# A preparation's inputs in another place, a new order of its TensorE work, and a gate bias loaded as rows

## The chip, the cores and the metric

The kernel runs on one core of one Trainium2 chip. The metric is the device time of one execution in microseconds; the time before is 2539.73 us, the median of three runs (2536.66 to 2539.75).

## The reference, cut to what matters

One layer works on x of 1024 tokens by 1024 channels, all in float32:

```
x = x + 0.5 * swiglu(rmsnorm(x, ff1_norm), ff1_w_gate, ff1_w_up, ff1_w_down)   # d_ff = 2816
h = rmsnorm(x, mix_norm)
a_in, q, k, v, g_logits = split(h @ w_in)
y_a = gmlp_spatial_gating(gelu(a_in), ...)
y_b = stick_breaking_attention(q, k, v)          # 16 heads of 64, strictly causal
g_a, g_b = split(sigmoid(g_logits + b_gate))     # b_gate: 2 * 1024
x = x + (g_a * (y_a @ w_branch_a) + g_b * (y_b @ w_branch_b)) @ w_out
x = x + 0.5 * swiglu(rmsnorm(x, ff2_norm), ff2_w_gate, ff2_w_up, ff2_w_down)
y = rmsnorm(x, final_norm)
```

## The kernel before, in words

Each float32 operand is split into a high and a low part (ScalarE casts the high part, VectorE or GpSimd subtracts it to get the low one), and each product is three matmuls: high times high, high times low, low times high (lines 67 to 69 for the mixer, 166 to 168 for the layer halves).

The program has three stages. `ffn` runs twice, as the first layer half (f1) and as the second (f2); `mixer` stands between them.

`ffn` multiplies by a Strassen-Winograd scheme with seven products instead of eight. It begins with a **preparation**. The eight row blocks t of x (128 tokens each) are normalized (`normed`, line 111: sum of squares on ScalarE, a power on GpSimd, one half of the row scaled on VectorE at line 116, the other multiplied by the weights on GpSimd at line 114 and scaled on ScalarE at line 117) and transposed on TensorE (line 177) into right operands: B11 and B21 from blocks 0 to 3 (`lo_forms`), and B22, T3, T1, T2, T4 from blocks 4 to 7 (`hi_forms`). For each of the blocks 4 to 7, `hi_forms` transposes first, and leaves two later steps, `second` and `third`. These add or subtract B11 or B21 with matmuls by a plus or minus unit matrix (line 199), each followed by a split into a T (lines 185 and 186); each step on the same bank can begin only when the split before it has read the bank.

Between these pieces TensorE works on **heads**: head f is the product of 128 columns of the gate weights with B11 (`pb`) and with B21 (`ba`), which `head_part` issues as parts of 12 matmuls of 512 columns (or two half parts of 256). The heads 0 to 3 are made in the preparation. After that `tail(f)` does the other products with T1 to T4 and B22 for each f, 22 in all, and stores sums for the second phase, the products with `wd` (tiles pf, wf, pd). In f1 all eight blocks are prepared; in f2 (`ready`) B11 and B21 come from the mixer, and only blocks 4 to 7 are left. The x of f2 is xres, which the mixer stores at its end (line 828).

In the preparation the order of TensorE and of SyncE, which issues all DMAs, is the written one; instructions written outside may still be placed between them. ScalarE, VectorE and GpSimd follow an order that a planner chooses at build time, each engine then in that order; outside such blocks it orders TensorE and SyncE as well, and may take an instruction ahead of earlier ones when its operands and buffers are free. An operand's buffer can be taken over tile by tile from a pool that has ended (`reuse_waits="tile"`).

The space of SBUF is a stack. Below lie `hp` (four operands of 16 KB per partition) and `wp` (two raw weight tiles, six forms wf). On these stands, in the layer halves, `bp` (two more raw tiles and two more forms, 16 KB), then `tp` (T3, T4 and B22, 48 KB), `pg` (8 KB) and on top `pre` (gain, three x tiles, xn, diff) and after it `pa` (the tails' tiles, 38 KB). For the second phase `pb` stands where tp, pg and pa stood. In the mixer `gp` (eight tiles of 2 KB for the v of attention, gates and parts of m) stands where bp stands, and on it attention's pool `ap` (90 KB) and, after attention, `u2` (42 tiles of 2 KB) and `np2` (10 KB and little tiles) in the same place.

In the mixer, banks of PSUM have tags: z and later projections use p0 (three banks), projections of q, k, v and the gates A use p1 (two), transposes p2 (two). The gates of the first four d are called before gMLP and write into gp, so they can run while attention does; their sigmoid (line 776) adds `bgate`, a tile that line 765 loads with 128 partitions of 16 single elements each.

Of the kernel before, what the change touches and what calls it, by code (L numbers as in the profile page):

```python
# [19 lines left out]
HALF = 512  # L20
# [3 lines left out]
XNF, XNB = 7, 5  # L24
# [8 lines left out]
class Kernel:  # L33
# [74 lines left out]
        nc.gpsimd.tensor_tensor(r[:, 1:2], r[:, 0:1], self.neghalf, op=ALU.pow)  # L108
        return r[:, 1:2]

    def normed(self, x, gain, tiles):

        nc = self.nc
        nc.gpsimd.tensor_tensor(tiles[1], x[1], gain[1], op=ALU.mult)  # L114
        r = self.rstd(x, tiles[0])
        nc.vector.scalar_tensor_tensor(tiles[0], x[0], r, gain[0], op0=ALU.mult, op1=ALU.mult)
        nc.scalar.activation(tiles[1], tiles[1], AF.Copy, scale=r)

    def gain(self, g):
        t = [self.utile("gain") for _ in range(2)]  # L120
# [102 lines left out]
    def ffn(self, xsrc, gain_src, wg, wu, wd, before, after, T=None):  # L223
# [13 lines left out]
        with ExitStack() as outer:  # L237
            fps = outer.enter_context(tc.tile_pool(name="fps", bufs=8, space=PSUM, reuse_waits="tile"))
            self.psum = lambda tag, name: fps.tile([P, HALF], F32, tag="ps", name=name)
            bp = outer.enter_context(tc.tile_pool(name="bp", bufs=1, reuse_waits="tile"))  # L240
            count = {"raw": 0, "wf": 0}

            def rawt():
                count["raw"] += 1
                own = count["raw"] % 2 == 0
                return (bp if own else self.wp).tile([P, D], F32, tag="raw", bufs=2, name="raw")

            def wform(src, sub=None):
                count["wf"] += 1
                own = count["wf"] % 4 == 0  # L250
                return self.form(bp if own else self.wp, "wf", 2 if own else 6, src, sub)


            with tc.tile_pool(name="tp", bufs=3, reuse_waits="tile") as tp, tc.tile_pool(name="pg", bufs=1, reuse_waits="tile") as pg:
                T = T or self.first_forms()
                for i, n in enumerate(("T2", "T1", "T3", "T4", "B22")):
                    T[n] = (self.hp if i < 2 else tp).tile([P, 4, 2, HALF], F32R, tag="h", name=n)
# [30 lines left out]
                    tt(glo, a, glo, op=ALU.add)  # L288
                    return gate, b, glo

                with tc.tile_pool(name="pre", bufs=1, reuse_waits="tile") as pre, tc.manual_schedule(engines={mybir.EngineType.PE, mybir.EngineType.SP}):
# [3 lines left out]
                    x, heads = {}, {}  # L295

                    def load(t):
                        x[t] = pre.tile([P, D], F32, tag="xr", bufs=3, name="xr")
                        nc.sync.dma_start(out=x[t], in_=xsrc[t * P:(t + 1) * P, :])

                    def norm(t):
                        xn = [tmp("xn", 4) for _ in range(2)]
                        self.normed(cut(x[t]), cut(gain), xn)
                        return xn

                    pool = nc.gpsimd.tensor_tensor
                    q = [slice(i * 256, (i + 1) * 256) for i in range(2)]
                    full = lambda f: heads.update({f: head_end(heads[f])})
                    if ready:
                        heads[0], heads[1] = head(0, pool), head(1, pool)  # L310
                        nc.sync.dma_start(out=gain, in_=gain_src.partition_broadcast(P))
                        for t in (4, 5, 6):
                            load(t)
                        work = {4: 0, 5: 1, 6: 2, 7: 3}
                    else:
                        load(0)
                        nc.sync.dma_start(out=gain, in_=gain_src.partition_broadcast(P))
                        load(1), load(2)
                        heads[0] = head(0, pool)
                        load(3)  # L320
                        heads[1] = head(1, pool)
                        self.lo_forms(0, norm(0), T)
                        self.lo_forms(1, norm(1), T)
                        head_part(heads[0], q[0])
                        load(4)
                        self.lo_forms(2, norm(2), T)
                        head_part(heads[1], q[0])
                        load(5)
                        self.lo_forms(3, norm(3), T)
                        load(6)  # L330
                        for f in range(2):
                            head_part(heads[f], q[1])
                            full(f)
                        work = {4: 2, 5: 3}
                    for t in range(4, NT):
                        f = work.get(t)
                        if f is not None and f not in heads:
                            heads[f] = head(f, pool)
                        xn = norm(t)
                        if ready:  # L340
                            head_part(heads[f], which=(2,))
                        second, third = self.hi_forms(t, xn, T, tmp)
                        if t == 4:
                            load(7)
                        if f is not None:
                            head_part(heads[f], which=(3,) if ready else (2,))
                            if ready:
                                full(f)
                        second()
                        if f is not None and not ready:  # L350
                            head_part(heads[f], which=(3,))
                            full(f)
                        third()

                with tc.tile_pool(name="pa", bufs=1, reuse_waits="tile") as pa:
                    tile = lambda tag, bufs: pa.tile([P, HALF], F32, tag=tag, bufs=bufs, name=tag)

# [55 lines left out]
                    for f in range(nff):  # L413
                        if f not in heads:
                            heads[f] = head(f)
                            head_part(heads[f])
                            full(f)
# [460 lines left out]
```

## Time and profile before

| | |
|---|---|
| median of three runs | 2539.73 us |
| the profiled execution | 2541.97 us |
| its span, from the first to the last instruction | 2540.2 us |
| TensorE matmul busy | 2451.0 us |
| VectorE, ScalarE, GpSimd busy | 1685.2, 1050.4, 350.0 us |
| mean granted clock of TensorE | 0.986 of full speed |
| preparation of f1, attention, preparation of f2 | from 0, to 1268.5, from 1851.5 us |

Busy time counts an instruction from its start to its modelled end; matmuls overlap, so a stretch in which TensorE is busy throughout can hold more or less work. In a timeline, a row gives start, length, engine, line and operation, and in brackets the idle time before it and what ended that.

### The profile page before, as it was taken

What the parts mean: (1) busy time and instruction counts of PE and PEld (TensorE: products, weight loads), DVE (VectorE), ACT (ScalarE), POOL (GpSimd) and SP (SyncE); (2) the same over time, 40 slices, a digit from 0 to 9 for tenths busy, and PEclk for the clock granted to TensorE, in tenths of its full rate; (3) what the DMA queues carried; (4) which work ended last, traced back from release to release, by engine and by line L of the source; (5) the groups of instructions that cost most, each with busy time, mean ns of one, the idle gap of its engine ahead of it and who ended that gap; (6) DMA issues with size and microseconds to landing.
All of it is one profiled execution on the core that took longest, in us unless ns stands there. A gap on an engine that the chain in (4) does not pass through costs nothing.

```text
span 2540.2 us, 33329 instructions
## 1 busy us (share of the span) xinstructions
PE 2451.0 (96%) x12268; PEld 2074.1 (82%) x12268; DVE 1685.2 (66%) x2595; ACT 1050.4 (41%) x1996; POOL 350.0 (14%) x510
## 2 busy tenths in 40 slices
PE   6999999999999999999999999999979999999998
PEld 5788888788889897988888888888857888887886
DVE  5877787565757888787675555145848777874655
ACT  6333333344646666665522222222334333333444
POOL 4000000000324445443200000000130000000002
PEclk9999999999999999999999999999989999999999
DMA  4553553775421212121111121123445535547653
GB/s 145 181 171 124 177 176 128 292 253 173 157 58 34 67 34 67 34 67 51 34 51 53 47 71 58 54 75 125 133 129 178 175 126 178 173 138 285 229 178 133
DMA packets 252771, 318.33 MB, mean 125 GB/s; under 512 B 14912, under 2 KB 172096, under 8 KB 252608
## 3 DMA queue, kind: packets, MB, share of 16 engines
q1 hardware_dynamic: 252608, 316.21, 38.4%
q8 instruction: 96, 1.57, 0.3%
q14 instruction: 67, 0.55, 0.1%
HBM read 227.55 MB, written 80.22 MB: 121 GB/s over the span
## 4 chain that ended last, share of the span: by engine, by line
PE 83%; DVE 7%; DMA 4%; issue 2%; ACT 1%; POOL 1%; SPq 0%; POOLq 0%; DVEq 0%; ACTq 0%
PE pj L67 7%; PE pj L68 7%; PE pj L69 7%; PE pd L168 7%; PE pd L167 7%; PE pd L166 7%; PE pb L167 4%; PE pb L166 4%; PE pb L168 4%; PE av L609 3%; PE pv L68 2%; PE pv L69 2%; PE pv L67 2%; PE tr L602 2%; PE pe L167 1%
## 5 line engine op out<-in xcount | busy, mean ns | idle before, releaser
L150 ACT CAST wf<-raw 128x512 fp32r<-128x512 f32 x280 | 166.7, 620 | 237.2 <-PE pd L168 99.1
L67 PE MATMUL pj<-h,wf 128*128 128x512 f32 x640 | 254.6, 398 | 5.7 <-DVE q L74 5.7
L151 DVE TENSOR_TENSOR wf<-raw,wf 128x512 fp32r<-128x512 f32 x264 | 178.0, 696 | 118.0 <-ACT wf L150 115.7
L68 PE MATMUL pj<-h,wf 128*128 128x512 f32 x640 | 253.3, 396 | 0.0
L69 PE MATMUL pj<-h,wf 128*128 128x512 f32 x640 | 252.8, 396 | 0.0
L57 DVE TENSOR_TENSOR wf<-raw,wf 128x1024 fp32r<-128x1024 f32 x88 | 108.3, 1231 | 143.3 <-ACT wf L56 142.8
L585 DVE TENSOR_TENSOR_SCAN kp<-kp 128x128 f32<-128x128 f32 (+7 forms) x128 | 179.9, 1413 | 33.5 <-POOL kp L583 32.0
L150 ACT CAST wf<-ws 128x512 fp32r<-128x512 f32 x176 | 107.9, 622 | 207.8 <-DVE ws L159 106.5
L56 ACT CAST wf<-raw 128x1024 fp32r<-128x1024 f32 x88 | 92.8, 1054 | 222.0 <-PE pj L68 121.1
L589 POOL TENSOR_TENSOR bt<-bt,kp 128x512 f32<-128x512 f32 (+4 forms) x128 | 129.8, 1015 | 139.9 <-DVE kp L585 119.4
L67 PEld LDWEIGHTS pj<-h,wf 128*128 128x128 f32 x640 | 122.1, 191 | 31.2 <-DVE q L74 7.0
L67 PE MATMUL pv<-wf,h 128*128 128x256 f32 x512 | 145.1, 285 | 2.1 <-ACT vg L652 2.1
L68 PE MATMUL pv<-wf,h 128*128 128x256 f32 x512 | 145.3, 284 | 0.6 <-DVE wf L57 0.6
L69 PE MATMUL pv<-wf,h 128*128 128x256 f32 x512 | 145.3, 284 | 0.0
L69 PEld LDWEIGHTS pj<-h,wf 128*128 128x128 f32 x640 | 121.9, 190 | 25.0 <-DVE wf L57 0.2
L68 PEld LDWEIGHTS pj<-h,wf 128*128 128x128 f32 x640 | 122.2, 191 | 24.2
L114 POOL TENSOR_TENSOR xn<-x,gain 128x512 f32<-128x512 f32 x12 | 16.8, 1406 | 893.9 <-DVE x L474 601.6
L166 PE MATMUL pb<-T,wf 128*128 128x512 f32 x352 | 137.5, 391 | 0.8 <-ACT pe L372 0.8
L167 PE MATMUL pb<-T,wf 128*128 128x512 f32 x352 | 137.0, 389 | 0.0
L168 PE MATMUL pb<-T,wf 128*128 128x512 f32 x352 | 136.9, 389 | 0.0
L166 PE MATMUL pd<-wf 128*128 128x512 f32 x344 | 133.1, 394 | 1.8 <-DVE x L463 1.6
L167 PE MATMUL pd<-wf 128*128 128x512 f32 x344 | 134.6, 391 | 0.0
(216 smaller groups left out, 6585.1 us busy)
## 6 DMA issues: line engine op xcount, KB each, us to landing
raw<-in_ff_w_down_dram SPq DMA_DIRECT2D x66, 512.0 KB, 6.3
raw<-in_w_in_dram SPq DMA_DIRECT2D x56, 512.0 KB, 3.9
raw<-in_ff_w_gate_dram SPq DMA_DIRECT2D x52, 512.0 KB, 4.4
raw<-in_ff_w_up_dram SPq DMA_DIRECT2D x44, 512.0 KB, 6.0
f_t2t<-as SPq DMA_DIRECT2D x22, 512.0 KB, 4.9
f_a11a<-act SPq DMA_DIRECT2D x44, 256.0 KB, 4.2
f_s2s<-as SPq DMA_DIRECT2D x22, 512.0 KB, 2.7
f_s3s<-as SPq DMA_DIRECT2D x22, 512.0 KB, 5.6
```

What stands on the lines that cost most here:

```text
L56: nc.scalar.copy(hi, raw)
L57: (nc.gpsimd if early else nc.vector).tensor_tensor(lo, raw, hi.bitcast(F32), op=ALU.subtract)
L67: mm(ps, lhsT=lh, rhs=rh, start=first, stop=False)
L68: mm(ps, lhsT=lh, rhs=rl, start=False, stop=False)
L69: mm(ps, lhsT=ll, rhs=rh, start=False, stop=last)
L150: self.nc.scalar.copy(f[:, 0, :], src)
L151: (sub or self.nc.vector.tensor_tensor)(f[:, 1, :], src, f[:, 0, :].bitcast(F32), op=ALU.subtract)
L166: mm(ps, lhsT=lh, rhs=rh, start=first, stop=False, skip_group_check=True)
L167: mm(ps, lhsT=lh, rhs=rl, start=False, stop=False, skip_group_check=True)
L168: mm(ps, lhsT=ll, rhs=rh, start=False, stop=last, skip_group_check=True)
L585: nc.vector.tensor_tensor_scan(rev, rev, rev, 1.0, op0=ALU.mult, op1=ALU.bypass)
L589: eng.tensor_tensor(bt[:, :n], bt[:, :n], kp[:, i * HALF + 1:i * HALF + 1 + n], op=ALU.mult)
```

## The change

Five edits. (1) Gain and the x tiles of a preparation get a pool `xp` of their own, which opens first, where gp stands in the mixer; `pre` keeps xn and diff, and `bp` opens only when both have closed, so that the preparation has two raw tiles and six forms instead of four and eight. (2) `tp` and `pg` stand at the other end of SBUF (`side="right"`). (3) For blocks 0 and 1 the second half of the row is normalized by one VectorE instruction. (4) TensorE and SyncE get a new order in the preparation: in f2 both parts of head 0 come before the first transposes, the third step of a block comes after the first of the next block, heads 2 and 3 lie one block later than in f1 before; in f1 the first two x tiles are loaded before gain. (5) `b_gate` is no longer loaded at the beginning of the mixer but behind attention, into a tile of np2 as 16 rows of 128, which TensorE transposes and VectorE copies to `bgate`.

```diff
-    def normed(self, x, gain, tiles):
+    def normed(self, x, gain, tiles, shared=True):
-        nc.gpsimd.tensor_tensor(tiles[1], x[1], gain[1], op=ALU.mult)
+        if shared:
+            nc.gpsimd.tensor_tensor(tiles[1], x[1], gain[1], op=ALU.mult)
         r = self.rstd(x, tiles[0])
         nc.vector.scalar_tensor_tensor(tiles[0], x[0], r, gain[0], op0=ALU.mult, op1=ALU.mult)
-        nc.scalar.activation(tiles[1], tiles[1], AF.Copy, scale=r)
+        if shared:
+            nc.scalar.activation(tiles[1], tiles[1], AF.Copy, scale=r)
+        else:
+            nc.vector.scalar_tensor_tensor(tiles[1], x[1], r, gain[1], op0=ALU.mult, op1=ALU.mult)
...
-            bp = outer.enter_context(tc.tile_pool(name="bp", bufs=1, reuse_waits="tile"))
-            count = {"raw": 0, "wf": 0}
+            bp, count = None, {"raw": 0, "wf": 0}
...
-                own = count["wf"] % 4 == 0
+                own = bp and count["wf"] % 4 == 0
...
-            with tc.tile_pool(name="tp", bufs=3, reuse_waits="tile") as tp, tc.tile_pool(name="pg", bufs=1, reuse_waits="tile") as pg:
+            right = lambda name, bufs: tc.tile_pool(name=name, bufs=bufs, side="right", reuse_waits="tile")
+            with right("tp", 3) as tp, right("pg", 1) as pg:
...
+                left = lambda name: tc.tile_pool(name=name, bufs=1, reuse_waits="tile")
+                with left("xp") as xp, left("pre") as pre, tc.manual_schedule(engines={mybir.EngineType.PE, mybir.EngineType.SP}):
-                    gain = pre.tile([P, D], F32, tag="gain", name="gain")
+                    gain = xp.tile([P, D], F32, tag="gain", name="gain")
...
                     if ready:
-                        heads[0], heads[1] = head(0, pool), head(1, pool)
-                        nc.sync.dma_start(out=gain, in_=gain_src.partition_broadcast(P))
-                        for t in (4, 5, 6):
-                            load(t)
+                        new_head(0)
+                        load_gain()
+                        load(4), load(5)
+                        new_head(1)
+                        load(6)
+                        norm(4)
+                        part(0, 2), part(0, 3)
                     else:
-                        load(0)
-                        nc.sync.dma_start(out=gain, in_=gain_src.partition_broadcast(P))
-                        load(1), load(2)
+                        load(0), load(1)
+                        load_gain()
+                        load(2)
...
+                    first(4)
+                    load(7)
+                    norm(5)
+                    if ready:
+                        part(1, 2)
+                        second(4)
+                        new_head(2)
+                        part(1, 3)
+                    else:
+                        part(1, 2, q[1])
+                        second(4)
+                        new_head(2)
+                        part(1, 3, q[1])
+                    first(5)
+                    norm(6)
+                    third(4)
+                    new_head(3)
+                    part(2, 2)
+                    second(5)
+                    part(2, 3)
+                    first(6)
+                    norm(7)
+                    third(5)
+                    part(3, 2)
+                    second(6)
+                    part(3, 3)
+                    first(7)
+                    third(6)
+                    second(7)
+                    third(7)
+
+                bp = outer.enter_context(left("bp"))
...
-        nc.sync.dma_start(out=bgate, in_=a["b_gate"][0].rearrange("(c p) -> p c", p=P))
         with tc.tile_pool(name="attn", bufs=2, reuse_waits="tile") as ap:
             self.attention(ap, ydram)
         with tc.tile_pool(name="u2", ...) as self.up, tc.tile_pool(name="np2", ...) as self.np_:
+            rows = self.np_.tile([16, P], F32, tag="xn", bufs=XNB, name="rows")
+            nc.sync.dma_start(out=rows, in_=a["b_gate"][0].rearrange("(c p) -> c p", p=P))
+            ps = self.psum("p2", "bg")
+            nc.tensor.transpose(ps[:, :16], rows, self.ident[:16, :16])
+            nc.vector.tensor_copy(bgate, ps[:, :16])
```

`first(t)` calls `hi_forms`, `second(t)` and `third(t)` its two later steps, and `part(f, n, cs)` is `head_part` for pb (n = 2) or ba (n = 3), over all 512 columns or over the half q[0] or q[1]. In f1, ahead of `first(4)`, the blocks 0 to 3 alternate with half parts of the heads 0 and 1.

## Rows read from the trace of the kernel before

**Rows 1.** The page, part 1: busy us, share of the span, instructions.
```profile
PE 2451.0 (96%) x12268; PEld 2074.1 (82%) x12268; DVE 1685.2 (66%) x2595; ACT 1050.4 (41%) x1996; POOL 350.0 (14%) x510
```

**Rows 2.** TensorE's waits, whole span: for whom, us in total, times, longest.
```profile
PE nt L177 <- DVE xn L116: 19.9, 3, 10.6
PE nt L199 <- DVE T L186: 14.5, 7, 4.7
PE pd L167 <- DVE pf L151: 8.1, 3, 3.1
...
PE pv L67 <- ACT vg L652: 2.1, 1, 2.1
```

**Rows 3.** Stretches: length, busy us of PE, PEld, DVE, ACT, POOL; clock, DMA, GB/s.
```profile
1851.40:1909.20 57.80, 39.26 (x170) 30.67 (x170) 26.57 (x45) 25.41 (x52) 18.41 (x16) 0.88 0.43 129
10.50:67.10 56.60, 46.12 (x250) 38.12 (x250) 36.20 (x61) 36.60 (x76) 27.15 (x25) 0.93 0.44 130
1640.00:1680.00 40.00, 40.00 (x178) 33.12 (x177) 12.82 (x18) 13.18 (x21) 0.00 (x0) 1.00 0.32 99
```

**Rows 4.** Timeline of TensorE, preparation of f2.
```profile
1851.47 0.47 PE L166 MATMUL pb<-B,wf 128*128 128x512 f32 x1 [0.88 <-DVE x L514]
...
1862.16 1.97 PE L177 MATMUL nt<-ident,xn 128*128 128x128 f32 x8 [7.71 <-DVE xn L116]
...
1879.44 1.04 PE L177 MATMUL nt<-ident,xn 128*128 128x128 f32 x8
...
1880.66 0.48 PE L166 MATMUL ba<-B,wf 128*128 128x512 f32 x1
...
1886.93 0.73 PE L199 MATMUL nt<-B,minus 128*128 128x512 f32 x2 [2.31 <-DVE T L186]
```

**Rows 5.** Timeline of SyncE ahead of the preparation of f2.
```profile
1841.83 9.84 SPq L828 DMA_DIRECT2D xres<-x  x8
...
1852.20 1.51 SPq L299 DMA_DIRECT2D xr<-xres  x3
```

**Rows 6.** Timeline of TensorE, preparation of f1.
```profile
27.36 0.39 PE L167 MATMUL pb<-B,wf 128*128 128x256 f32 x1 [2.13 <-DVE B L186]
```

**Rows 7.** Timelines of GpSimd, VectorE and SyncE, preparation of f1.
```profile
6.56 2.64 POOL L114 TENSOR_TENSOR xn<-xr,gain 128x512 f32<-128x512 f32 x2 [5.19 <-DMA gain<-in_ff_norm_dram]
...
9.75 0.75 DVE L116 SCALAR_TENSOR_TENSOR xn<-xr,rs,gain 128x512 f32<-128x512 f32 x1
...
17.28 1.76 DVE L116 SCALAR_TENSOR_TENSOR xn<-xr,rs,gain 128x512 f32<-128x512 f32 x1 [0.69 <-POOL rs L108]
...
3.33 1.56 SPq L765 DMA_DIRECT2D bgate<-in_b_gate_dram  x1
10.59 0.34 SPq L299 DMA_DIRECT2D xr<-in_x_dram  x1
```

**Rows 8.** Timelines of ScalarE and SyncE around the end of attention.
```profile
1180.76 0.68 ACT L776 ACTIVATE gate<-pj,bgate 128x512 f32<-128x512 f32 x1
...
1269.07 0.66 ACT L652 ACTIVATE vg<-pv 128x256 f32<-128x256 f32 x2
...
1238.10 0.37 SPq L54 DMA_DIRECT2D raw<-in_w_branch_a_dram  x1
```

**Rows 9.** The chain that ended last, around the end of attention: start, length, what.
```profile
1269.64 4.60 DMA wsraw<-in_gmlp_w_s_dram
```

**Rows 10.** Stretches of attention as in rows 3; rows two and three: tiles pj, pv.
```profile
1180.80:1268.50 87.70, 86.62 (x512) 76.10 (x510) 57.94 (x63) 45.99 (x95) 29.47 (x51) 1.00 0.14 38
...
1180.80:1268.50 87.70, 53.65 (x215) 39.36 (x215) 0.00 (x0) 4.88 (x7) 1.00 0.14 38
...
1180.80:1268.50 87.70, 6.98 (x48) 6.46 (x48) 0.00 (x0) 0.00 (x0) 1.00 0.14 38
...
885.00:948.00 63.00, 61.02 (x434) 57.12 (x434) 53.68 (x66) 40.40 (x89) 28.52 (x51) 0.97 0.16 36
```

**Rows 11.** The page, part 5: a group's busy us, mean ns, idle before.
```profile
L57 DVE TENSOR_TENSOR wf<-raw,wf 128x1024 fp32r<-128x1024 f32 x88 | 108.3, 1231 | 143.3 <-ACT wf L56 142.8
```

More of the change, by code (lines that the diff above doesn't have):

```diff
@@ L293, in ffn, with load_gain @@
                     self.np_ = pre
-                    gain = pre.tile([P, D], F32, tag="gain", name="gain")
-                    x, heads = {}, {}
+                    gain = xp.tile([P, D], F32, tag="gain", name="gain")
+                    x, xn, heads, rest = {}, {}, {}, {}
                     def load(t):
-                        x[t] = pre.tile([P, D], F32, tag="xr", bufs=3, name="xr")
+                        x[t] = xp.tile([P, D], F32, tag="xr", bufs=3, name="xr")
                         nc.sync.dma_start(out=x[t], in_=xsrc[t * P:(t + 1) * P, :])
+                    def load_gain():
+                        nc.sync.dma_start(out=gain, in_=gain_src.partition_broadcast(P))
@@ L301, in norm @@
                     def norm(t):
[L302 to L308, printed above, removed]
-                    if ready:
-                        heads[0], heads[1] = head(0, pool), head(1, pool)
-                        nc.sync.dma_start(out=gain, in_=gain_src.partition_broadcast(P))
-                        for t in (4, 5, 6):
-                            load(t)
-                        work = {4: 0, 5: 1, 6: 2, 7: 3}
-                    else:
-                        load(0)
-                        nc.sync.dma_start(out=gain, in_=gain_src.partition_broadcast(P))
-                        load(1), load(2)
-                        heads[0] = head(0, pool)
+                        xn[t] = [tmp("xn", 4) for _ in range(2)]
@@ new lines, in norm, with new_head, part, first @@
+                        self.normed(cut(x[t]), cut(gain), xn[t], t > 1)
+                    def new_head(f):
+                        heads[f] = head(f, nc.gpsimd.tensor_tensor)
+                    def part(f, n, cs=slice(0, HALF)):
+                        head_part(heads[f], cs, (n,))
+                        if n == 3 and cs.stop == HALF:
+                            heads[f] = head_end(heads[f])
+                    def first(t):
+                        rest[t] = self.hi_forms(t, xn.pop(t), T, tmp)
@@ new lines, in ffn @@
+                    second, third = (lambda t, i=i: rest[t][i]() for i in range(2))
+                    if ready:
+                        new_head(0)
[5 more added lines that the diff above has]
+                        part(0, 2), part(0, 3)
+                    else:
+                        load(0), load(1)
+                        load_gain()
+                        load(2)
+                        new_head(0)
@@ L320, in ffn @@
                         load(3)
[L321 to L324, printed above, removed]
+                        new_head(1)
+                        q = [slice(i * 256, (i + 1) * 256) for i in range(2)]
+                        norm(0), norm(1)
+                        self.lo_forms(0, xn.pop(0), T)
                         load(4)
-                        self.lo_forms(2, norm(2), T)
@@ L327, in ffn @@
-                        head_part(heads[1], q[0])
+                        norm(2)
+                        self.lo_forms(1, xn.pop(1), T)
+                        part(0, 2, q[0]), part(0, 3, q[0])
                         load(5)
-                        self.lo_forms(3, norm(3), T)
+                        norm(3)
+                        self.lo_forms(2, xn.pop(2), T)
+                        part(1, 2, q[0]), part(1, 3, q[0])
                         load(6)
-                        for f in range(2):
-                            head_part(heads[f], q[1])
-                            full(f)
@@ L334, in ffn @@
[L334 to L353, printed above, removed]
+                        norm(4)
```

7 lines of the change are left out of this document (4 added, 3 removed).

## The prediction

> **What bounds the kernel now.** I read the page's busy times first. TensorE is busy for 2451.0 us of a span of 2540.2 us [rows 1], so only its gaps, its slow clock and the order of its work can move the time. The list of what TensorE waited for came next: its largest entries are 19.9 us for normalized rows (xn) in front of the first transposes, 14.5 us for the split of the right operands T in front of the small unit matmuls, and 8.1 us for pf forms [rows 2]. The first two belong to the two preparations, so I took the table of stretches there: in 10.5 to 67.1 us TensorE is busy 46.12 of 56.60 us at a granted clock of 0.93, in 1851.4 to 1909.2 us 39.26 of 57.80 at 0.88, where a steady stretch has 178 matmuls of 512 columns in 40.00 us at 1.00, which is 0.225 us for each [rows 3]. The timelines of the second and the first preparation follow [rows 4 to 7], and at last the end of attention, where the load of the gate bias comes to stand [rows 8 to 11].
>
> **Base of the sum.** The profiled execution took 2541.97 us (span 2540.20, 1.77 around it), 2.24 above the median of 2539.73. Each sum below starts at 2541.97 and ends 2.24 lower.
>
> **Second preparation: -17 us.** TensorE's own need: eight parts (four heads, two each) of 12 matmuls, 96 x 0.225 = 21.6; four times 12 transposes, 1.22 us each time (1879.44 to 1880.66 [rows 4]), 4.9; 24 unit matmuls, 24 x 0.225 = 5.4. Together 31.9 us. The stretch from the first part (1851.47 [rows 4]) to where the tails run without gaps takes 57.8 [rows 3], so 25.9 us are waits and slow clock. Where they come from: the eight xres stores end at 1851.67 (1841.83 + 9.84) and the x loads go only at 1852.20, three at once [rows 5], so xn(4) is there at 1862.16 after a wait of 7.71, and the third step of a row block then waits for a split with nothing in front of it (2.31 at 1886.93) [rows 4]. The change lets gain and x(4) go to the space of the gates, whose last user is the first half of the output projection's second pass; x(4) then depends on its own store alone, the first of the eight. From the load to the transposes are 10.0 us today (1852.20 to 1862.16); with its load at about 1845, some 3 us behind the first store, xn(4) is there at about 1855. In front of the first transposes now stand two parts, 5.4 us from 1851.5, so to 1856.9: no wait. The third step gets a part and the next block's transposes ahead of it, 2.7 + 1.2 = 3.9 us against the 2.3 that it waited. What is late next: at block 7 four heads hold a bank each, the third head's sum another, d of block 6 one and the transposes want three, nine of eight, so about 1.5 us; after the last part nothing covers block 7's splits, 5; and 2 for in-order queues on ScalarE and VectorE, where casts of weights stand in front of splits. 25.9 - 8.5 = 17. Bounds: -8 (only the 7.71 goes) to -22.
>
> **First preparation: -8 us.** Need: 21.6 + 4.9 + 5.4, and four times eight transposes, about 3.5: 35.4 us; taken from 10.5 to 67.1 are 56.6 [rows 3]. The heads 2 and 3 now spread over blocks 5 and 6 instead of 4 and 5, so the last blocks are covered. I keep 3.6 for the slow clock at the start, 1.5 of the 2.13 at 27.36 [rows 6], 2 at block 4 (a half part is all that stands in front of its second step), 5 at the end and 2 for queues: 14.1. The start itself moves little. Today two products on GpSimd (2.64 us from 6.56, when gain has landed) stand in front of the power, and xn(0) begins on VectorE at 9.75 [rows 7]; now gain lands one load later, behind x(1), but the power no longer queues behind the products: I take 1.2 of the 2.64 as kept. 21.2 - 14.1 + 1.2 = 8. Bounds: -1 to -13.
> The price inside this step: each of blocks 0 and 1 adds one product to VectorE, 0.75 us alone, 1.76 where a GpSimd product ran beside it [rows 7]; two of them, 1.5 to 3.5, are in the 1.2. The Trainium skill (SBUF, State Buffer; Who interferes with whom) says that a VectorE instruction with two SBUF inputs and a GpSimd instruction that reads SBUF shut each other out; 0.75 against 1.76 agrees, and by that rule all four products beside the weights' low parts would take the whole 1.2 and 2 us more.
>
> **Right operands at the other end: +2 us.** The tails' tiles now lie where the first tiles of the down products will be, instead of three operand tiles that end earlier. TensorE waits 8.1 us in three places for pf today [rows 2]. If the first pf tile now waits for the stores of the last sums, this grows by up to 3 us in each layer half; if not, nothing. 0 to +6, and I take +2, near the end at which another buffer is taken.
>
> **Gate bias as rows: +34 us.** What goes is a load at 3.33 us that takes 1.56 us of SyncE [rows 7]. The next load in that queue waits for a buffer until 10.59 [rows 7], so it costs nothing now and gives nothing back. What matters is where the new load stands. It fills a tile of np2, a pool that shares its space with attention's. Of everything in that pool and in u2, nothing starts today before attention's last store: the first np2 load (wsraw) goes at 1269.64 [rows 9], while a load of W_A, written far later in the program but into free buffers, went at 1238.10, and the Gelu that empties the first pv bank begins at 1269.07 [rows 8] though pv's matmuls, 48 in this stretch, had filled both banks before [rows 10]. So I expect the rows at about 1269 less what attention gains, and the bias 3 us after.
> But the gates' sigmoids need that bias, and four gates (eight halves of 24 matmuls) run inside attention's last heads today: the second half's sigmoid is at 1180.76 [rows 8]. Without it two halves fill the two p1 banks and stop. The next three gates' weights hold all six wf buffers, so nothing else gets weights either. In 1180.8 to 1268.5 today 215 matmuls of pj and 48 of pv (half as wide) run: 215 x 0.225 + 48 x 0.112 = 53.7 us, which leaves 34.0 for the heads; VectorE is busy 57.94, of which four forms of 1.23 go, so 53 [rows 10, 11]. How fast can heads go alone? Not below 53; not above the 87.7 of today. The largest share that VectorE has in a stretch of attention is 53.68 of 63.00, 0.85, of seven that I looked at [rows 10]: 53 / 0.85 = 62 us. TensorE idles 62 - 34 = 28 us of these, and the 53.7 are done later. At the end TensorE has nothing while y is copied, summed and stored, the rows land (wsraw took 4.60 behind other loads [rows 9], I take half), and transpose, copy and sigmoid follow: some 5.5 us, an estimate, against the 2.1 that it waits there today for the Gelu [rows 2]; and a share of heads at a low clock, as in both preparations [rows 3], 3 us more. 28 + 3.4 + 3 = 34. Bounds: 0 (rows early) and 53.7 + 3.4 = 57 (heads no faster than today).
>
> **Sum.** 2541.97 - 17 - 8 + 2 + 34 = 2553, less 2.24: 2551 us.
>
> **Rivals.**
> *Rows come early* (ends on the other side). If np2's first tile is taken where attention's tiles don't reach, the bias is there before the gates and the term of 34 is 0: 2541.97 - 23 - 2.24 = 2517. For it: the rest of the kernel reuses space tile by tile (x loads 0.53 us behind the last store [rows 5]). Against it: wsraw is the same pool's first tile today and came at 1269.64 [rows 9]. It decides for faster as soon as the term is under 18.
> *Other work fills in.* The p0 banks take three halves of u as today; 72 x 0.225 = 16.2 us of the 28 are filled, and the slow clock goes: 28 - 16 + 3 = 15, so 2541.97 - 23 + 15 - 2.24 = 2532, faster. For it: those 72 matmuls run today before attention ends. Against it: they need weights, and gates written earlier come first to the buffers.
> *The preparations save little.* VectorE and ScalarE, which the planner orders, are late at every step, as at 27.36 and 1886.93 [rows 4, 6]: 8 us instead of 25, so 2541.97 - 8 + 2 + 34 - 2.24 = 2568.
>
> **How the numbers follow.** Forecast 0.64 (own range 2538 to 2566), rows early 0.10, filled in 0.16, little saved 0.10. A measurement of this kernel can tell 0.2%, 5 us. Slower by more: 0.74 of the forecast, all of the last rival, a little of the second, 0.58. Faster by more: the first rival, most of the second, little of the forecast, 0.25. Within: 0.17. The range 2520 to 2574 leaves out the first rival (0.10) and, above, heads that go no faster than today.
>
> **What would show it.** Second preparation: transposes of block 4 at about 1857 on the old scale, behind two parts, and no wait over 2.5 us for xn or T. First: tails without gaps some 8 us earlier. Gates: two sigmoids or none before attention's last store, the other gates' after it, and TensorE at about half in the last 60 us of attention; eight sigmoids before that store refute the forecast, and so does a rows load before it. The pf wait at the start of the down products grows or stays. The time is wrong if the heads alone need much more or less than 62 us.

## The result, and the profile after

The changed kernel takes 2566.35 us (median of four runs, 2564.40 to 2567.01) against 2539.24 us before on the same chip: the ratio is 1.0106, 95% interval [1.0093, 1.0118], 27.1 us slower. The forecast was +11: its direction and its range (2520 to 2574) hold, its size does not. The profiled execution took 2564.40 us, against 2541.97 before, so the two traces can show 22.4 us; the other 4.7 lie between profiled executions and medians.

TensorE's row of the page after; its busy time grew by 10.4 us [rows 1]:

```profile
PE 2461.4 (96%) x12269; PEld 2081.7 (81%) x12269; DVE 1686.0 (66%) x2598; ACT 1047.6 (41%) x1994; POOL 349.0 (14%) x508
```

What TensorE waited for, after (sum in us, times, longest):

```profile
PE pd L170 <- ACT pf L154: 18.3, 3, 8.8
PE nt L181 <- DVE xn L117: 17.6, 4, 8.6
PE nt L203 <- DVE T L190: 6.2, 3, 3.5
PE bg L805 <- DMA rows<-in_b_gate_dram: 4.1, 1, 4.1
```

The waits for T fell from 14.5 to 6.2 and those for xn only from 19.9 to 17.6 [rows 2]. The wait for pf forms, 8.1 and 2.2 us in two entries before, is now the largest. To place the loss, I read where TensorE starts the same piece of work in both traces:

| start of | before | after | offset | in between |
|---|---|---|---|---|
| last tail product, f1 | 472.22 | 471.02 | -1.2 | first preparation: -1.2 |
| first transposes after the down products, f1 | 667.06 | 669.35 | +2.3 | places: +3.5 |
| first attention score (z) | 737.45 | 739.62 | +2.2 | -0.1 |
| first part of the second preparation | 1851.47 | 1882.91 | +31.4 | bias as rows: +29.2 |
| last tail product, f2 | 2313.42 | 2334.42 | +21.0 | second preparation: -10.4 |
| end of the last matmul | 2530.77 | 2554.14 | +23.4 | places: +2.4 |

**Bias as rows.** SyncE, TensorE and ScalarE at the end of attention, after:

```profile
1185.72 57.92 SPq L651 DMA_DIRECT2D ydram<-y  x6
1243.73 0.53 SPq L803 DMA_DIRECT2D rows<-in_b_gate_dram  x1
```
```profile
1245.88 0.25 PE L805 MATMUL bg<-ident,rows 16*128 16x16 f32 x1 [4.05 <-DMA rows<-in_b_gate_dram]
```
```profile
1246.38 1.26 ACT L814 ACTIVATE gate<-pj,bgate 128x512 f32<-128x512 f32 x2 [3.94 <-DVE bgate L806]
```

The rows go behind attention's last store, and no gate's sigmoid runs before 1246.38; before, the second half's was at 1180.76 [rows 8]. Busy time of the engines in three stretches of attention, after (PE, PEld, DVE, ACT, POOL; clock, DMA, GB/s); the third is the stretch of [rows 10], moved by the 2.2 us that the later work had slipped, up to the last store:

```profile
1170.00:1200.00 30.00, 24.14 (x140) 19.44 (x138) 25.28 (x27) 18.77 (x43) 15.50 (x27) 1.00 0.13 35
1200.00:1230.00 30.00, 21.58 (x122) 17.74 (x122) 26.64 (x31) 19.40 (x45) 17.99 (x28) 0.89 0.06 14
...
1183.00:1243.20 60.20, 42.41 (x241) 34.36 (x240) 50.36 (x58) 35.33 (x79) 30.49 (x49) 0.89 0.08 20
```

One of these stretches before:

```profile
1200.00:1230.00 30.00, 30.00 (x168) 26.07 (x167) 22.29 (x24) 16.69 (x35) 12.03 (x21) 1.00 0.16 45
```

TensorE, full in the first two before, is busy 24.14 and 21.58 of 30 us; VectorE is busy for 0.84 and 0.89 of the time. From 1144 to 1262 us TensorE's gaps sum to 23.0. Attention ends 25 us earlier, and the gates and projections that ran inside it before are done afterwards.

**Second preparation.** TensorE, ScalarE and SyncE, after:

```profile
1882.91 0.47 PE L170 MATMUL pb<-B,wf 128*128 128x512 f32 x1 [0.88 <-DVE x L547]
1894.50 1.97 PE L181 MATMUL nt<-ident,xn 128*128 128x128 f32 x8 [5.89 <-DVE xn L117]
1925.17 0.73 PE L203 MATMUL nt<-B,plus 128*128 128x512 f32 x2 [1.35 <-DVE T L190]
```
```profile
1887.37 1.14 ACT L154 CAST wf<-raw 128x512 fp32r<-128x512 f32 x2 [15.25 <-DMA raw<-in_ff_w_gate_dram]
1890.15 0.58 ACT L291 COPY glo<-pb 128x512 f32<-128x512 f32 x1 [1.65 <-DMA xres<-x]
1890.64 0.63 ACT L104 ACTIVATE xn<-xr 128x512 f32<-128x512 f32 x1
```
```profile
1876.75 0.32 SPq L304 DMA_DIRECT2D xr<-xres  x1
1881.74 0.32 SPq L304 DMA_DIRECT2D xr<-xres  x1
1882.11 0.43 SPq L265 DMA_DIRECT2D raw<-in_ff_w_gate_dram  x1
```

The waits in front of the third steps of blocks 4 to 6 are gone (2.31 us for block 5 before [rows 4]; these are the other two of before):

```profile
1873.60 1.22 PE L199 MATMUL nt<-B,minus 128*128 128x512 f32 x2 [4.66 <-DVE T L186]
...
1896.93 0.73 PE L199 MATMUL nt<-B,minus 128*128 128x512 f32 x2 [1.53 <-DVE T L186]
```

x(4) is loaded at 1876.75, 6 us ahead of the first part, and yet block 4's transposes wait 5.89 us. ScalarE takes the squares of block 4 (1890.64) only after two casts of head 1, whose weights SyncE sent for behind x(5), and after the copy to glo (the tile for a head's sums), whose new place is one where x tiles of the mixer are still being stored. From the first part to where the tails run without gaps the granted clock is 0.89 of full speed, 0.88 before [rows 3]:

```profile
1882.91:1931.00 48.09, 38.84 (x172) 30.56 (x172) 26.63 (x46) 25.59 (x54) 20.55 (x18) 0.89 0.49 149
```

**First preparation.** Three engines again, after:

```profile
36.77 1.22 PE L203 MATMUL nt<-B,plus 128*128 128x512 f32 x2 [3.54 <-DVE T L190]
```
```profile
33.27 1.14 ACT L154 CAST wf<-raw 128x512 fp32r<-128x512 f32 x2 [3.44 <-DMA raw<-in_ff_w_gate_dram]
34.32 0.58 ACT L189 CAST B<-nt 128x512 fp32r<-128x512 f32 x1
```
```profile
26.81 10.05 SPq L265 DMA_DIRECT2D raw<-in_ff_w_gate_dram  x3
```

The pattern is the same: head 2's load (26.81) stands behind x(7), which waits for a buffer almost until then; head 2's casts stand ahead of block 4's splits on ScalarE, and TensorE waits 3.54 us for these. The tails run without gaps from 66.85 us (67.07 before).

**Places.** The start of f1's down products, after:

```profile
480.14 2.08 PE L170 MATMUL pd<-pf 128*128 128x512 f32 x4 [8.72 <-ACT pf L154]
```
```profile
478.94 4.26 ACT L154 CAST pf<-raw 128x512 fp32r<-128x512 f32 x8 [7.88 <-DMA f_s3s<-as]
```

The first pf tile lies over a tile of the last left sums (as, which the tails store for the second phase), and the cast waits until that is stored. TensorE loses 8.72 us, 8.79 in f2. The same place before:

```profile
473.35 1.21 PE L166 MATMUL pd<-pf 128*128 128x512 f32 x4 [0.73 <-ACT pf L150]
...
477.63 0.80 PE L167 MATMUL pd<-pf 128*128 128x512 f32 x1 [3.08 <-DVE pf L151]
```

### The profile page after: what moved, and what is told of

It reads as the page before. It is cut to its first block, busy times and chain, and to the rows that moved or that the text cites. A ratio compares the mean times of both kernels' runs of the same rounds, so it can differ in the third digit from the quotient of the medians.

```text
span 2562.5 us, 33322 instructions
## 1 busy us (share of the span) xinstructions
PE 2461.4 (96%) x12269; PEld 2081.7 (81%) x12269; DVE 1686.0 (66%) x2598; ACT 1047.6 (41%) x1994; POOL 349.0 (14%) x508
## 4 chain that ended last, share of the span: by engine, by line
PE 88%; DVE 6%; issue 2%; DMA 1%; ACT 1%; POOL 1%; SPq 0%; POOLq 0%; ACTq 0%; DVEq 0%
PE pd L170 8%; PE pd L172 8%; PE pd L171 8%; PE pj L67 7%; PE pj L68 7%; PE pj L69 7%; PE pb L172 5%; PE pb L171 5%; PE pb L170 5%; PE av L642 2%; PE pv L69 2%; PE pv L67 2%; PE pv L68 2%; PE tr L635 2%; PE pe L172 2%
## 5 line engine op out<-in xcount | busy, mean ns | idle before, releaser
L57 DVE TENSOR_TENSOR wf<-raw,wf 128x1024 fp32r<-128x1024 f32 x88 | 108.3, 1230 | 177.6 <-ACT wf L56 177.3
```

Source lines behind the costliest of these rows:

```text
L57: (nc.gpsimd if early else nc.vector).tensor_tensor(lo, raw, hi.bitcast(F32), op=ALU.subtract)
```

## The experiments

Each ratio is to the kernel before, run again beside it; its median lay between 2538.95 and 2539.76 us each time, so the medians are compared directly below. The changed kernel took 2566.35.

| kernel | us | to before, interval |
|---|---|---|
| bias by columns as before | 2535.88 | 0.9987 [0.9978, 0.9997] |
| rows early | 2536.38 | 0.9989 [0.9980, 0.9999] |
| no bias | 2536.20 | 0.9989 [0.9979, 0.9998] |
| rows alone on before | 2570.86 | 1.0122 [1.0108, 1.0136] |
| head 1 first, glo at the end | 2562.65 | 1.0092 [1.0077, 1.0107] |
| and squares first | 2560.88 | 1.0084 [1.0069, 1.0100] |
| old order, x in gates' space | 2567.36 | 1.0115 [1.0100, 1.0130] |
| f1: head 2 ahead of x(7) | 2562.38 | 1.0095 [1.0080, 1.0110] |
| f1: bp first | 2566.53 | 1.0109 [1.0094, 1.0124] |
| ws behind | 2564.30 | 1.0099 [1.0084, 1.0114] |
| places apart | 2554.52 | 1.0057 [1.0044, 1.0071] |
| all but places | 2527.80 | 0.9951 [0.9938, 0.9965] |
| all, rows early | 2513.47 | 0.9897 [0.9883, 0.9910] |
| all, bias by columns | 2510.24 | 0.9891 [0.9875, 0.9908] |

### The bias: four runs

```diff
+        nc.sync.dma_start(out=bgate, in_=...rearrange("(c p) -> p c", p=P))
         with tc.tile_pool(name="attn", ...) as ap:
...
-            rows = self.np_.tile([16, P], ...)    # and its load, transpose, copy
```


> The changed kernel with the gate bias loaded as before, by columns at the start of the mixer; everything else as changed. Theory (the gates' sigmoids wait for a load whose tile lies in attention's space, and that costs about 30 us; the second preparation began 31.4 us later than before): about 2536 us, the first gate sigmoids again near 1170 to 1180 us, attention's last store again near 1268 us. Rival (the late second half is due to the other parts, and the gates only trade places with the heads): over 2555 us.

The time is 2535.88 us, 30.5 less than the changed kernel. These are the first and the last of eight gate sigmoids on ScalarE, all inside attention again (its last store is at 1270.82):

```profile
1173.86 0.69 ACT L810 ACTIVATE gate<-pj,bgate 128x512 f32<-128x512 f32 x1 [0.52 <-PE pj L69]
...
1237.31 0.74 ACT L810 ACTIVATE gate<-pj,bgate 128x512 f32<-128x512 f32 x1
```

Next, the rows are kept, but come early:

```diff
+        rows = self.wp.tile([P, 1024], F32, tag="raw", bufs=2, name="raw")[:16, :P]
+        ...                                       # load, transpose, copy, ahead of attention
         with tc.tile_pool(name="attn", ...) as ap:
```


> The changed kernel with the rows of the gate bias loaded and transposed before attention, into a buffer of the raw weights that is free there, instead of into a tile that shares attention's space. Theory (the place of the tile, not the form of the load, is what costs): within 2 us of the run with the old load by columns, about 2536 us. Rival (the transpose on TensorE and the copy out of a bank cost by themselves, or take a raw buffer at a bad time): 2541 us or more.

The time is 2536.38 us, 0.5 from the load by columns and within the spread of the executions: loading rows and transposing them is not what costs. This edit moves the tile and the load's place in the program together. What speaks for the tile's place is that before the change a load of W_A, written far later but into a free buffer, went at 1238.10, ahead of attention's last store [rows 8]; no run moves the tile alone.

The third run leaves the bias out of the sigmoids, and its output lacks it:

```diff
-  AF.Sigmoid, bias=bgate[:, row + d:row + d + 1])
+  AF.Sigmoid)
```


> The changed kernel without the bias in the gates' sigmoids (the output then lacks b_gate); the rows are still loaded into the tile in attention's space and transposed behind attention. Theory (the cost of the rows is the gates' wait for them, and the two banks and six weight buffers that waiting gates hold): the gates run inside attention again and 25 to 29 us come back, 2537 to 2541 us; the 4 us that TensorE waits for the load at attention's end may stay. Rival (the load and the transpose in the middle of TensorE's order at attention's end cost by themselves): 2555 us or more.

The time is 2536.20 us. The rows still land late, and TensorE still waits for them:

```profile
1273.43 0.21 PE L805 MATMUL bg<-ident,rows 16*128 16x16 f32 x1 [3.62 <-DMA rows<-in_b_gate_dram]
```

But the gates run inside attention, and the whole 30 us are back, 1 more than expected. So the late load and its transpose cost nothing by themselves that can be told; the rival falls, and the cost is the gates' wait for the bias.

The fourth run takes the kernel before and changes the load of the bias alone:

> The kernel before with the one part that loads the gate bias as rows behind attention. Theory (the cost of the rows does not depend on the other parts): 29 to 31 us more than before, 2569 to 2571 us. Rival (it needs the space of the gates to be held, or the first layer's different end): 2560 us or less, or 2575 or more.

The time is 2570.86 us, 31.4 over its before (2539.49). The cost does not hang on the other parts of the change.

### The second preparation: three runs

```diff
-            with right("tp", 3) as tp, right("pg", 1) as pg:
+            with right("pg", 1) as pg, right("tp", 3) as tp:
...
+                        new_head(1)
                         load_gain()
                         load(4), load(5)
-                        new_head(1)
```


> The changed kernel with two edits in the second preparation: the weights of head 1 are loaded ahead of gain and the x tiles as before, and the tile for the sums of the heads (glo) lies at the far end of SBUF instead of over the x tiles of the output projection. Theory (ScalarE takes its work in order, and the squares of block 4 stand behind the casts of head 1, whose weights land at 1887, and behind the copy to glo, which waits until 1890 for the last store of x): the 5.89 us in front of block 4's transposes fall under 1 us and the time by about 5, to 2561 us. Rival (xn(4) is bound by its own x tile, its stores and its loads): the wait stays over 4 us and the time at 2566.

The time is 3.7 us less; which of the two edits gave it was not tried. TensorE still waited 2.58 us for xn(4): the copy to glo, released at 1886.45 by the first part's sums, still stood ahead of the squares. So the next edit writes ScalarE's order out:

```diff
+                        with tc.manual_schedule(engines={mybir.EngineType.Activation}):
-                        norm(4)
-                        part(0, 2), part(0, 3)
+                            norm(4)
+                            part(0, 2), part(0, 3)
```


> The two edits of the second preparation together (head 1's weights ahead of gain and x, glo at the far end), and ScalarE's order there written out so that the squares of block 4 come ahead of the copy to glo. Theory (with those edits alone TensorE still waited 2.58 and 0.69 us for block 4, because the squares stood behind the copy, which waits for the first part's sums at 1886.4): no wait over 1 us in front of block 4's transposes, the first tail product 3 us earlier than in that run against the preparation's start (37 to 38 us behind it instead of 40.7), about 2559.5 us. Rival (something later in the preparation, the weights of heads 2 and 3 or the splits, then sets its end): the waits move there, 2562 to 2563 us.

TensorE there:

```profile
1881.49 0.47 PE L170 MATMUL pb<-B,wf 128*128 128x512 f32 x1 [0.88 <-DVE x L548]
1887.33 1.09 PE L181 MATMUL nt<-ident,xn 128*128 128x128 f32 x8 [0.16 <-DVE xn L117]
1918.81 0.80 PE L170 MATMUL pd<-T,wf 128*128 128x512 f32 x1 [1.04 <-ACT wf L154]
```

In this trace the wait is 0.16 us, and the first tail product comes 37.32 us behind the first part, against 55.20 before, 44.03 after and 40.74 with the first two edits. To the last tail product the gain over before is 17.2 us, the forecast's size. But the traced execution took 2556.53 us and is the fastest of four (up to 2562.40); the granted clock in these 37.32 us is 1.00. The median, 2560.88, is 1.4 above the number expected and 1.8 under the run with two edits, too little to tell theory from rival. The version "all but places" below has the same second preparation, and its trace has 40.07 us at a granted 0.96, a gain of 14.5 to the last tail product, and this wait:

```profile
1857.43 1.09 PE L181 MATMUL nt<-ident,xn 128*128 128x128 f32 x8 [1.96 <-DVE xn L117]
```

The last of the three keeps the first two edits and puts the order of TensorE and SyncE of before back:

```diff
+                        for t in range(4, NT):
+                            ...
+                            norm(t); part(t - 4, 2); first(t)
+                            ...
+                            part(t - 4, 3); second(t); third(t)
```


> The second preparation with x and gain in the gates' space as in the change, but with TensorE's and SyncE's order of before (both first heads' weights ahead of gain and x; in each row block norm, part, transposes, part, second and third step), glo at the far end; everything else as changed. It stands beside the run with the same two edits and the new order (2562.65 us; from the preparation's start to its last effect on the tails 13.7 us shorter than before). Theory (the place of x is worth the wait of 7.71, the order is worth the waits in front of the third steps): about 7 to 8 us shorter than before, waits of 1.5 to 4.7 us in front of the minus matmuls again, 2568 to 2570 us. Rival (the place is all of it): 2562 to 2564 us.

```profile
1886.32 0.47 PE L170 MATMUL pb<-B,wf 128*128 128x512 f32 x1 [0.88 <-DVE x L549]
1893.67 1.97 PE L181 MATMUL nt<-ident,xn 128*128 128x128 f32 x8 [4.38 <-DVE xn L117]
1903.98 0.72 PE L203 MATMUL nt<-B,minus 128*128 128x512 f32 x2 [2.25 <-DVE T L190]
1914.32 0.72 PE L203 MATMUL nt<-B,minus 128*128 128x512 f32 x2 [1.88 <-DVE T L190]
1924.31 0.73 PE L203 MATMUL nt<-B,minus 128*128 128x512 f32 x2 [1.53 <-DVE T L190]
1934.05 0.49 PE L170 MATMUL pd<-T,wf 128*128 128x512 f32 x1 [1.25 <-ACT wf L154]
```

The waits in front of the third steps are back, and of the 7.71 us in front of block 4's transposes 4.38 stay. To the first tail product it takes 47.73 us, 7.5 less than before; the new order takes another 7.0 off (40.74). But the tails begin at full clock here: in their first 20 us 85 matmuls run at a granted 1.00, before 73 at 0.91, after 70 at 0.83. So to the last tail product, where before took 461.95 us, the place (with the two edits) has gained 10.1 and the new order 3.6 more, and the medians of the two runs (2567.36 and 2562.65) differ by 4.7. The changed kernel itself gained 10.4 to this point: with head 1's load and glo where the change puts them, its new order is worth hardly more than the old order with both put right. The median is 0.6 under the range expected.

### The first preparation: two runs

```diff
                         part(0, 2, q[1]), part(0, 3, q[1])
+                        new_head(2)
                     first(4)
                     load(7)
...
-                        new_head(2)
```


> The changed kernel with one edit in the first preparation: the weights of head 2 are loaded ahead of x(7), not behind it. Theory (in-order queues: the load stands behind x(7), which waits for an x buffer until 26.8 us; its casts stand ahead of block 4's splits on ScalarE, and TensorE waits 3.54 us at 36.77 for them): that wait falls under 1.5 us, the first tail product comes at about 61 instead of 64.4 us, the time falls by 2 to 3 us to about 2563.5. Rival (the end of the preparation, block 7's splits and the sums of weights that wait for its tiles, sets the start of the tails anyway): the first tail product stays at 64 and the time at 2566.

The time is 4.0 us less, more than expected. The first tail product comes at 59.03 instead of 64.38 us, and this is TensorE's wait in the same place:

```profile
33.04 0.73 PE L203 MATMUL nt<-B,plus 128*128 128x512 f32 x2 [0.17 <-DVE T L190]
```

The second run gives the first preparation its extra weight buffers back:

```diff
+                bp = None if ready else outer.enter_context(left("bp"))
                 with left("xp") as xp, ...
```


> The changed kernel with the second space for weights (bp: two more raw buffers and two more for forms) opened ahead of the first preparation, as before the change, with x and gain behind it; the second preparation keeps its x in the gates' space. Theory of the order on SyncE: the load of head 2 still stands behind x(7), so the wait of 3.54 us stays and the time at 2565 to 2566. Rival (the change took the preparation's extra weight buffers, and that is where its gain went): the loads of the weights come earlier, the first tail product at 62 us or before, 2563 us or less.

The time is 2566.53 us, as the changed kernel's, with a wait of 2.99 us in place of 3.54: the buffers are not what costs. The first tail product came at 63.16, the last no earlier (-0.9 against before; -1.2 as changed).

### The places: two runs

```diff
-  with tc.tile_pool(name="pa", ...) as pa:
+  with left("pa") as pa, left("pw") as pw:       # ws from pw
```


> The changed kernel with the operand sums (ws) of the tails in a pool of their own behind the tails' other tiles, so that the first pf tile of the down products lies over ws, which are read last before the last product, and no longer over the tiles of the left sums (as), which still have to be stored. Theory (the first pf cast waits for the store of as, 8.72 and 8.79 us of TensorE's time instead of 0.73 + 3.08): the two waits fall back to 3 to 4 us each and the time by 9 to 11, to about 2556 us. Rival (the casts of pf are late because their raw weights land late, or the buffers at 165 to 172 KB are not what they wait for): the waits stay at 8 to 9 us and the time at 2566.

This expectation half failed: the pf waits are back at 0.73 and 3.09 us, but the time, 2564.30, fell by 2 us only, where 9 to 11 were expected. SyncE at that place:

```profile
475.73 0.32 SPq L429 DMA_DIRECT2D f_s3s<-as  x1
476.16 6.58 SPq L493 DMA_DIRECT2D x<-in_x_dram  x6
482.78 0.53 SPq L468 DMA_DIRECT2D raw<-f_a11a  x1
```

The six x loads (3.91 us before, 4.38 as changed) now take 6.58 us, behind the stores of the left sums, and the next weights go behind them. So I gave both places of their own:

```diff
+  with left("pz") as pz, left("pc") as pc, left("pa") as pa, left("pw") as pw:  # as, gs; act; pe; ws
...
+  with left("pb") as pb, left("pq") as pq, right("px", 1) as px:               # rw, gain, xn; pf; x
```


> The changed kernel with the tiles of the tails and of the down products placed apart: the left sums (as) where the down products' rw tiles lie, ws and pe where the first pf tile lies, and the x tiles at the other end, over the right operands. Theory (what the changed places cost is two waits for stores of as: of the first pf cast, and, when only that one is taken away, of the x loads, which stand ahead of the raw loads in SyncE's queue: 3.91 us before, 6.58 us in the run with ws behind): both go, the offset from the last tail product to the end of the down products falls from +3.5 and +2.4 us against the kernel before to under 1 in both layers, the time to about 2561 us. Rival (the start of the down products is bound by transfers, whose share is 0.97 to 1.00 there, so what is saved at one wait comes back at the next): 2564 us or more, as with ws behind.

The time is 2554.52 us, 11.8 less than the changed kernel and twice what was expected. From the last tail product of f1 to the first transposes it takes 190.4 us, 194.8 before, 198.3 after; in f2, to the end of the last matmul, 213.3, 217.4 before, 219.7 after. The last tail product itself came later than as changed, by 2.0 us in f1 and by 2.3 behind the preparation's start in f2, which takes part of it back. Its eight x loads go ahead of the left sums' stores, VectorE splits the first pf tile before the left sums, and the two waits for pf are 0.71 and 0.60. These are 20 us from the first pf product on (first the length, TensorE's busy time and matmuls; the granted clock is the third number from the end):

```profile
474.09:494.09 20.00, 19.40 (x83) 15.55 (x84) 11.39 (x19) 7.16 (x14) 0.00 (x0) 1.00 1.03 408
```

The same stretch before:

```profile
473.35:493.35 20.00, 16.93 (x62) 13.47 (x63) 10.36 (x17) 5.45 (x10) 0.00 (x0) 0.83 0.97 365
```

How the excess divides between the transfers' order, VectorE's order and the clock was not tried.

### Together

> The changed kernel with the mends that measured faster, all but the places of the tails' tiles: rows of the bias ahead of attention (30 us), head 2's weights ahead of x(7) (4), and the three edits of the second preparation (5.5). Theory (the parts add): 2566.4 - 30 - 4 - 5.5 = 2527 us. Rival (some of them share a gain, as the two later ones, which both come out of the first preparation's end and the edit of glo's place): 2530 us or more.

The time is 2527.80 us, as the sum said.

> The version with all mends, and the tiles of the tails and of the down products placed apart as well. Theory (the places cost 5 to 6 us in the two layers): 5 us under the version without, about 2522 us. Rival (transfers bound the start of the down products): within 2 us of the version without.

The time is 2513.47 us, 14.3 less: the places again gave more than expected.

> The version with all mends, with the bias loaded by columns as before instead of as rows ahead of attention. Theory (the rows, once they are early, cost TensorE a transpose and a raw buffer, and the attention of the run with them began 1.4 us later than that with columns): 1 to 3 us under the version with early rows (2513.5 us). Rival (no cost that can be measured): within 1 us.

The median is 2510.24 us, 3.2 less and just past what was expected; but two of the four executions with early rows took 2510.75 and 2511.28, inside the spread here (2509.61 to 2511.39), so a cost of the rows is not shown. This is the lowest median: 28.7 us under its before (2538.95).

## Why the prediction was right in direction and wrong in size

- *Gate bias as rows, +34*: right, a little high. The traces give 29.2, the two pairs of runs 30.5 and 31.4. The mechanism stands step by step: the rows behind the last store, no gate's sigmoid before that, and the heads alone in 60.2 us where 62 were forecast, with VectorE busy for 0.84 of it where 0.85 was assumed. The division was otherwise: of these 60.2 us TensorE idled 17.8, not 28, and took 42.4 at a granted 0.89 for the work that was put at 34.0. The low clock is thus inside the 60.2 us, and the 3 us that the sum added for it on top do not show.
- *Second preparation, -17*: -10.4. The load of x(4) went where the sum put it (1876.75, which is 1845.3 on the old scale; 1845 was forecast). The step that failed comes next: "xn(4) is there at about 1855", and with it the term "2 for in-order queues on ScalarE and VectorE". The sum carried 10.0 us over from that load to block 4's transposes; they took 17.8, behind a wait of 5.89 us that the sum put at nothing. The price had been seen on casts in front of splits; it fell on casts and a copy in front of block 4's squares. That glo's new place delays its copy was not seen: of the right operands' move only the down products were weighed. The sum also kept nothing here for a slow clock, and the granted clock was 0.89. With casts and copy moved, one trace gives -17.2, the fastest of four executions, at a granted 1.00; another with the same preparation gives -14.5 at 0.96. So most of what was missing is found, and the last 2 to 3 us hang on the execution, for a reason that no run shows.
- *First preparation, -8*: -1.2. The same term, 2 us for queues, failed: the new place of head 2's load in SyncE's order was not followed through, though the order of the other loads was, and block 4's wait of 3.54 us came of it, with a granted clock of 0.87 from 33 to 59 us (1.00 with the load moved). Undone, the term is -6.0; the other 2 us stay open. TensorE began 2.0 us earlier where 1.2 was forecast. The product on VectorE took 0.75 us, and 1.75 where it ran beside a GpSimd product (from 10.19 and 10.12 us on), much as [rows 7] show. The Trainium skill (SBUF, State Buffer; Who interferes with whom) has the two shut each other out, and that agrees. The 2 us more that the prediction worked out by that rule did not come, since only one of the four products met a GpSimd product.
- *Right operands, +2*: +3.5 and +2.4, 5.9 in all. The mechanism was named (the first pf tile waits for the stores of the last sums), but the term was mis-sized: up to 3 us in each half were allowed, +2 in all was taken, and almost the whole 6 came. No run takes this edit back alone; the two runs on places show that the places are what costs.
- *Sum*: forecast -17 - 8 + 2 + 34 = +11; traced -10.4 - 1.2 + 5.9 + 29.2 = +23.5, less 0.1 ahead of attention and 1.1 behind the last matmul: 22.3, the difference of the spans.
- *Rivals*: the rows did not come early, and no other work filled in (from 1200 to 1230 us no projection ran). The third, "the preparations save little", held 0.10 and comes nearest: the two preparations saved 11.6 us instead of 25, and its 2568 us lies within 2 of the time measured. Its reason holds in part: ScalarE was late in front of one row block of each preparation, not at every step. That the direction came out right is owed to the bias, whose term outweighs the other three.

## What to carry to other kernels

When loads or head products move in a written order, follow each of them through the queues of the engines that the planner orders: what a moved load releases late stands ahead of what TensorE needs next. When pools move, list for each new tile what lay in its place and when that is stored, for the first tile of every stage; a small tile that early work depends on (here 512 bytes per partition of bias) can hold up the most. When a move of tiles costs time, try a third placement and not only the old one: here the move cost 5.9 us by the traces, and a third placement took 11.8 off again, which by these two numbers is about 6 us under the old one.

## What the runs showed of the hardware

In these runs a wait cost TensorE more than its length, since the granted clock fell to the lower of its two levels, 1.2 and 2.4 GHz, behind it for a while. In the first 20 us of f1's down products 62 matmuls ran at a granted 0.83 on the mean, behind waits of 0.73 and 3.08 us, and 83 at 1.00, behind 0.71 and 0.60: 2.5 us less of waiting gave 21 matmuls more, 4.7 us at 0.225 each. In the first preparation the removal of a 3.54 us wait brought the first tail product 5.4 us forward. The clock fell behind short waits too: in the run with the squares first, waits of 1.35, 1.04, 0.56 and 0.41 us stand within 7 us at the start of f2's tails, and from 1919 to 1925 us the granted clock is 0.50. The 20 us behind the second of these waits, with the clock third from the end:

```profile
1918.81:1938.81 20.00, 19.03 (x70) 14.75 (x71) 15.77 (x26) 7.66 (x14) 0.00 (x0) 0.83 0.64 191
```
